# Sums of the heads' outputs by accumulating stores, one ring of six for weight blocks and pooled tiles, and one product order for every pair

## The chip, the cores and the metric

The kernel runs on one core of one Trainium2 chip. The metric is the device time of one execution in microseconds, the median of several runs. TensorE (PE) multiplies, VectorE (DVE) and ScalarE (ACT) make operands and take results, GpSimd (POOL) does small work, SyncE (SP) issues almost all transfers.

## What is computed

The reference is one decoder block on 1024 tokens of width 1024, all in float32:

```python
q, f_pre, i_val, o_gate, pool_v, gate_a, gate_b = split(x @ w_in)
a = HGRN2(q, f, i_val)             # gated recurrence, 8 heads of 128, chunks of tokens
a = (rms_norm(a) * g * sigmoid(o_gate)) @ w_a
b = (causal_mean(pool_v) - pool_v) @ w_pool(per group) * pool_scale
x = LN(alpha * x + (sigmoid(gate_a) * a + sigmoid(gate_b) * b) @ w_out)
x = LN(alpha * x + relu(x @ w_up)**2 @ w_down)
```

## The kernel before

Every large product is done in three passes (high by high, high by low, low by high part), so that float32 accuracy comes from TensorE's faster 32-bit form. `split` (L123) makes the two parts of an operand: ACT casts the high part (L125), DVE subtracts it (L126).

The large products are also done by a seven-product scheme. `pair` (L270) computes two blocks of 128 output columns for both halves of the tokens. From four weight blocks b11, b12, b21, b22 and seven sets of token sums it makes seven **products** p1 to p7. One product (`prod`, L203) is 12 matmuls of 128x512: L208, L210, L211, four times. The products of a pair go into three PSUM banks: **a** takes p1, and later p6, p5 and p3 on top; **c** takes p2; **z** takes p7, and later p4 on top. Between the additions the bank is read: after p1, ACT copies a (`copied`, L276, the copy is L278); after p7 it copies z; after p6 it copies a again; after p5, DVE adds a to the copy of z (`added`, L281, the addition is L282); after p3 the bank holds the last output. The next product onto a bank has to wait until that reading is done.

There are two orders. With `twin` false, p1 p2 p6 p7 p5 p4 p3: the banks alternate. With `twin` true, p1 p2 p7 p4 p6 p5 p3: z twice running, then a three times running; that order is used where `run` (L366) is given two pairs, whose products alternate, so that the banks alternate again (`a_pair`, L1077, and the first two pairs of the up projection, L1257).

The stages, in order:

- the values of the heads (L443 to L583);
- **the recurrence stage** (L1023 to L1034): ORDER (L33) lists inputs of the heads, pooled channels, output gates and gates, each one pair with `twin` false, run alone. After each product `run` advances the generator `recurrence` by one turn (L380), which at two turns of about 8.5 puts the recurrence's small matmuls between the products. In this stage the order of TensorE's instructions is as written (`manual_schedule`, L1025); the other engines' orders, and TensorE's in all other stages, are set by a scheduler when the kernel is built;
- what is left of the recurrence's turns (L1033), then `pool_products` for group 0, `gates(6)`, `pool_products` for groups 1 to 3 and `gates(7)` (L1035);
- the product with w_a on two pairs at a time (L1091 to L1113), for which `o_operand` (L606) loads the heads' outputs and their sums;
- the product with w_out, the first layer norm, the up projection in 16 pairs (L1259 to L1293) and the down projection.

What the change touches besides: `raw_tile` (L213) is a ring of two tiles of 4 KB per partition, two blocks each, and differences of blocks go to a ring "t" of two (L247). The parts of operands go to a ring of 10 tiles, NW, which is five products' worth. `turn_outputs` (L973) stores each head's output of each half to DRAM (L979) from the tile "og", of which there is one; the next half's `outputs` (L955) loads its gate into that same tile (L957). `o_sums` (L614) loads four of those stores back for each of four block rows, makes s3, s2, s1, s4 with four DVE operations (L617 to L620) in tiles of the ring "c", and stores them (L622). The copies L278 of the pairs use ring "c" too. `pool_products` (L717) loads w_pool into "tA" and the pooled tiles into "q", "f", "og" and "v" (L725, L728).

Of the kernel before, what the change touches and what calls it, by code (L numbers as in the profile page):

```python
# [9 lines left out]
F32 = mybir.dt.float32  # L10
# [6 lines left out]
P = 128  # L17
# [18 lines left out]
    ("gates", 2), ("inputs", 7), ("pooled", 3), ("gates", 3), ("gates", 4), ("gates", 5),  # L36
# [14 lines left out]
def tile_hybrid_block(  # L51
# [126 lines left out]

    def first_tokens(name, *tags):
# [33 lines left out]
    def raw_tile():  # L213
        return wq.tile([P, CH, 2, P], F32, tag="raw", name=nm("raw"), bufs=2)

    def w_blocks(src, c1, c2, tile_of=raw_tile):

        raw = tile_of(), tile_of()

        def load(*which):  # L220
            for kh in range(2):
                rows_of = src[kh * HALF : (kh + 1) * HALF, :].rearrange("(k p) c -> p k c", p=P)
                if c2 == c1 + P and len(which) == 2:
                    done = nc.sync.dma_start(
                        out=raw[kh].rearrange("p k n c -> p k (n c)"), in_=rows_of[:, :, c1 : c1 + 2 * P]
                    )
                else:
                    for n in which:
                        c = (c1, c2)[n]
                        done = nc.sync.dma_start(out=raw[kh][:, :, n], in_=rows_of[:, :, c : c + P])  # L230
            return done

        return raw, load

    def loaded_blocks(*args):
        raw, load = w_blocks(*args)
        load(0, 1)
        return raw
# [6 lines left out]

    def w_diff(a, b):
        t = wq.tile([P, CH, P], F32, tag="t", name=nm("t"), bufs=2)  # L247
        V.tensor_sub(t, a, b)  # L248
        return t
# [20 lines left out]
    def pair(raw, rooms, takes, pz_tag="pj", twin=False, pc_tag="pj"):  # L270


        b11, b12, b21, b22 = raw if len(raw) == 4 else (raw[kh][:, :, n] for kh in range(2) for n in range(2))
        c, ps = {}, {}

        def copied(room, ps):  # L276
            t = room()
            A.copy(t, ps)  # L278
            return t

        def added(t, ps):  # L281
            V.tensor_add(t, t, ps)  # L282
            return t

        def t3():
            c["t"] = w_diff(b22, b12)
            return w_part(c["t"])

        def t2():
            if not twin:  # L290
                V.tensor_add(c["t"], c["t"], b11)
            return w_part(c["t"])

        def t4():
            if not twin:
                V.tensor_sub(c["t"], b21, c["t"])
                return w_part(c["t"])
            V.tensor_add(c["t"], c["t"], b11)
            V.tensor_sub(b21, b21, c["t"])
            return w_part(b21)  # L300

        def t1():
            return w_part(w_diff(b12, b11))

        def p1(w):
            ps["a"] = ps_tile()
            prod(ps["a"], w, "a11", True)
            c[11] = copied(rooms[0], ps["a"])

        def p2(w):  # L310
            ps["c"] = ps_tile(pc_tag, 4 if pc_tag == "pj" else 2)
            prod(ps["c"], w, "a12", True)

        def p7(w):
            ps["z"] = ps_tile(pz_tag, 4 if pz_tag == "pj" else 2)
            prod(ps["z"], w, "s3", True)
            with tc.high_priority(PRIO):
                takes[0](added(c[11], ps["c"]))
                c[22] = copied(rooms[2], ps["z"])

        def p6(w):
            prod(ps["a"], w, "s2", False)
            with tc.high_priority(PRIO):
                c[21] = copied(rooms[1], ps["a"])
                if twin:
                    takes[2](added(c[21], ps["z"]))

        def p4(w):
            prod(ps["z"], w, "a22", False)
            if not twin:  # L330
                with tc.high_priority(PRIO):
                    takes[2](added(c[21], ps["z"]))
# [20 lines left out]
        return (  # L353
            ((t0,), ((t0, p1),)),
            ((b_21,), ((b_21, p2),)),
            *(
                (((t3,), ((t3, p7),)), ((t4,), ((t4, p4),)), ((t2,), ((t2, p6),)), ((t1,), ((t1, p5),)))
                if twin
                else (((t3, t2), ((t2, p6), (t3, p7))), ((t1, t4), ((t1, p5), (t4, p4))))
            ),  # L360
            ((b_22,), ((b_22, p3),)),
        )
# [48 lines left out]
    with tc.tile_pool(name="xr", bufs=8, side="right", reuse_waits="tile") as xr:  # L411
# [11 lines left out]
        g_col, pscale = prm[:, 16:24], prm[:, 24:32]  # L423
        lb = const.tile([P, 8], F32, name="lb")
# [29 lines left out]
        def raw_tile_rows():  # L454
            return [raw_tile().rearrange("p k n c -> p (k n c)").rearrange("p (k c) -> p k c", c=HALF) for _ in range(2)]
# [138 lines left out]
    def raw_rows(src, k2, cc):  # L594

        raw = raw_tile().rearrange("p k n c -> p (k n c)").rearrange("p (k c) -> p k c", c=HALF)
        rows_of = src[k2 * P : (k2 + 2) * P, cc * HALF : (cc + 1) * HALF].rearrange("(k p) c -> p k c", p=P)
        nc.sync.dma_start(out=raw, in_=rows_of)
# [15 lines left out]
    def o_sums(kp, tile_of=c_tile):  # L614

        a11, a21, a12, a22 = (loaded(od[k][u], tile_of) for k, u in ((kp, 0), (kp, 1), (kp + CH, 0), (kp + CH, 1)))
        V.tensor_add(a22, a21, a22)  # L617
        V.tensor_sub(a21, a11, a21)
        V.tensor_sub(a11, a22, a11)
        V.tensor_sub(a12, a12, a11)  # L620
        for name, t in zip(("s3", "s2", "s1", "s4"), (a21, a11, a22, a12)):
            nc.sync.dma_start(out=osd[name][kp], in_=t)  # L622

# [3 lines left out]
    with tc.tile_pool(name="tmp", bufs=1, side="right", reuse_waits="tile") as tmp:  # L627
# [89 lines left out]
        def pool_products(g):  # L717

            tags = iter(("q", "f", "og", "v") * 3)

            def room(dtype=F32):
                return tt(next(tags), dtype)

            raw = tt("tA").rearrange("p (k c) -> p k c", c=2 * P)
            nc.sync.dma_start(out=raw, in_=w_pool[g].rearrange("(k p) c -> p k c", p=P))  # L725
            wh, wl = split(raw, lambda: room(F32R).rearrange("p (k c) -> p k c", c=2 * P))
            for u in range(2):
                pl = [split(loaded(pod[2 * g + i][u], room), row_tile) for i in range(2)]  # L728
                for i in range(2):
                    w = slice(i * P, (i + 1) * P)  # L730
                    j = 2 * g + i
                    t = room() if j == KT - 1 else loaded(gbd[j][u], room)
# [88 lines left out]
        class Half:  # L821
# [151 lines left out]
            def turn_outputs(self):  # L973
# [4 lines left out]
                V.scalar_tensor_tensor(self.og, pt, g_col[:, self.h : self.h + 1], self.og, ALU.mult, ALU.mult)  # L978
                nc.sync.dma_start(out=od[self.h][self.u], in_=self.og)  # L979

        def recurrence():
# [10 lines left out]
            for n in range(2 * HEADS + 1):  # L992
# [11 lines left out]
                for turn in range(1, round(at) - round(at - PER_HALF)):  # L1004
                    if turn == TURN_BACK:
# [18 lines left out]
        head_inputs(0, (None, None, "p6", None, None))  # L1024
        with tc.manual_schedule(engines={mybir.EngineType.PE}):  # L1025
# [9 lines left out]
            for what, j in (  # L1035
                ("pool_products", 0), ("gates", 6), ("pool_products", 1), ("pool_products", 2), ("pool_products", 3), ("gates", 7),
# [40 lines left out]
        def a_pair(p):  # L1077
            raw = loaded_blocks(w_a, 2 * p * P, (2 * p + 1) * P, raw_tile if p % 2 else mg_raw)
            room = mg_tile("room", 4)
            takes = [gated(2 * p + i, u, p < 2) for u in range(2) for i in range(2)]  # L1080
            return pair(raw, (c_tile, room, room), takes, "hg", True)
# [76 lines left out]
    with tc.tile_pool(name="wo", bufs=1, side="right", reuse_waits="tile") as mp:  # L1158
        st1 = [None] * 8
        g1, b1 = ln_params(lambda: f(act_tile()).rearrange("p a b -> p (a b)"), ln1_g, ln1_b)  # L1160
        for k2 in range(0, KT, 2):
            raw = raw_rows(w_out, k2, 1)
            for k in range(2):
                n = len(wo)
                out_row(raw[:, k], (
# [46 lines left out]
    with tc.tile_pool(name="up", bufs=1, side="right", reuse_waits="tile") as up:  # L1212
# [15 lines left out]
        def units(i, raw):  # L1228
# [28 lines left out]
            return pair(raw, (c_tile,) * 3, (take(0), last, take(2), take(3)), "hg", i < 2, "tr" if i == 2 else "pj")  # L1257

        def up_blocks(i):  # L1259
            return w_blocks(w_up, i * 2 * P, i * 2 * P + P, up_raw_tile if i % 2 else raw_tile)  # L1260

        blocks = [up_blocks(i) for i in range(2)]
        for _, load in blocks:
            load(0, 1)
        pairs = [units(i, raw) for i, (raw, _) in enumerate(blocks)]
# [21 lines left out]
        for i in range(3, NP):  # L1287
            raw, load = up_blocks(i)
            w_load = load(0, 1)
            if i == NP - 2:  # L1290
                for part in down_rows(0, ws0):
                    part(w_load)
# [185 lines left out]
```

## Time and profile before

| what | value |
|---|---|
| median of the runs | 1476.05 us (1474.28 to 1478.21) |
| the profiled execution's own time | 1478.48 us |
| its span, first to last instruction | 1476.5 us |
| mean granted TensorE clock | 0.991 |
| PE busy | 1439.8 us, 98% |
| DVE busy | 1113.2 us, 75% |
| ACT busy | 759.3 us, 51% |
| POOL busy | 82.3 us, 6% |
| transferred | 226.82 MB, mean 154 GB/s |

The span is 1.98 us shorter than the execution's own time; this lies around it. PE is busy nearly all the time, so the place to look is the remaining 36.7 us in which it is not, and the stretches in which its granted clock is below 1.

### The profile page before, as it was taken

What the parts mean: (1) busy time and instruction counts of PE and PEld (TensorE: products, weight loads), DVE (VectorE), ACT (ScalarE), POOL (GpSimd) and SP (SyncE); (2) the same over time, 40 slices, a digit from 0 to 9 for tenths busy, and PEclk for the clock granted to TensorE, in tenths of its full rate; (3) what the DMA queues carried; (4) which work ended last, traced back from release to release, by engine and by line L of the source; (5) the groups of instructions that cost most, each with busy time, mean ns of one, the idle gap of its engine ahead of it and who ended that gap; (6) DMA issues with size and microseconds to landing.
All of it is one profiled execution on the core that took longest, in us unless ns stands there. A gap on an engine that the chain in (4) does not pass through costs nothing.

```text
span 1476.5 us, 20702 instructions
## 1 busy us (share of the span) xinstructions
PE 1439.8 (98%) x7377; PEld 1191.5 (81%) x7377; DVE 1113.2 (75%) x1822; ACT 759.3 (51%) x1383; POOL 82.3 (6%) x260
## 2 busy tenths in 40 slices
PE   9999999999999998789999999999999999999997
PEld 7887888888878886668788888888888888888886
DVE  5967877887897895458986589666666787777978
ACT  5445566666655654446542357555555543343435
POOL 0002111111110100000002100000000100000000
PEclk9999999999999999999999999999999999999999
DMA  6232233233234336687764134444464874535422
GB/s 249 76 117 93 63 103 122 72 122 122 65 128 160 127 116 220 192 297 271 244 211 160 57 115 164 157 147 151 146 238 168 274 267 135 170 132 169 137 72 114
DMA packets 160615, 226.82 MB, mean 154 GB/s; under 512 B 11232, under 2 KB 84480, under 8 KB 160512
## 3 DMA queue, kind: packets, MB, share of 16 engines
q1 hardware_dynamic: 158576, 218.93, 44.1%
q0 software_dynamic: 1152, 4.19, 0.8%
q10 hardware_dynamic: 784, 2.38, 0.5%
q8 instruction: 58, 0.95, 0.3%
q14 instruction: 45, 0.37, 0.1%
HBM read 154.16 MB, written 71.30 MB: 153 GB/s over the span
## 4 chain that ended last, share of the span: by engine, by line
PE 86%; DVE 6%; DMA 5%; ACT 2%; issue 1%; SPq 0%; DVEq 0%; ACTq 0%
PE ps_pj L208 14%; PE ps_pj L210 14%; PE ps_pj L211 14%; PE ps_pj L1360 4%; PE ps_pj L1361 4%; PE ps_pj L1359 4%; PE ps_pj L113 2%; PE ps_pj L112 2%; PE ps_pj L114 2%; PE ps_tr L1360 1%; PE ps_tr L1361 1%; PE ps_tr L1359 1%; PE ps_sc L208 1%; DMA og<-po 1%; PE ps_sc L211 1%; PE ps_sc L210 1%
## 5 line engine op out<-in xcount | busy, mean ns | idle before, releaser
L208 PE MATMUL ps_pj<-act,w 128*128 128x512 f32 x1068 | 421.8, 396 | 10.3 <-ACT c L278 6.0
L211 PE MATMUL ps_pj<-act,w 128*128 128x512 f32 x1068 | 416.4, 391 | 0.1
L210 PE MATMUL ps_pj<-act,w 128*128 128x512 f32 x1068 | 415.9, 391 | 0.5 <-DVE act L131 0.5
L208 PEld LDWEIGHTS ps_pj<-act,w 128*128 128x128 f32 x1068 | 201.5, 189 | 56.5 <-ACT c L278 7.4
L211 PEld LDWEIGHTS ps_pj<-act,w 128*128 128x128 f32 x1068 | 201.5, 189 | 43.5 <-DVE w L126 0.5
L210 PEld LDWEIGHTS ps_pj<-act,w 128*128 128x128 f32 x1068 | 201.7, 189 | 41.6 <-DVE act L131 0.9
L125 ACT CAST w<-t 128x512 fp32r<-128x512 f32 x170 | 105.7, 622 | 139.0 <-PE ps_pj L210 82.5
L125 ACT CAST w<-raw 128x512 fp32r<-128x512 f32 x143 | 88.7, 622 | 129.0 <-PE ps_pj L210 79.7
L126 DVE TENSOR_TENSOR w<-t,w 128x512 fp32r<-128x512 f32 x170 | 116.3, 686 | 38.1 <-ACT w L125 37.6
L126 DVE TENSOR_TENSOR w<-raw,w 128x512 fp32r<-128x512 f32 x143 | 99.8, 701 | 57.3 <-ACT w L125 56.1
L1321 ACT CAST act<-act 128x1024 fp32r<-128x1024 f32 x66 | 67.0, 1050 | 107.6 <-issue 35.0
L1360 PE MATMUL ps_pj<-act,act 128*128 128x512 f32 x240 | 92.9, 389 | 0.0
L1361 PE MATMUL ps_pj<-act,act 128*128 128x512 f32 x240 | 92.9, 389 | 0.0
L1359 PE MATMUL ps_pj<-act,act 128*128 128x512 f32 x240 | 92.4, 389 | 0.0
L1322 DVE TENSOR_TENSOR act<-act,act 128x1024 fp32r<-128x1024 f32 x66 | 79.2, 1219 | 16.5 <-ACT act L1321 16.4
L282 DVE TENSOR_TENSOR c<-c,ps_pj 128x512 f32<-128x512 f32 x95 | 64.7, 682 | 30.9 <-PE ps_pj L211 24.8
L278 ACT COPY c<-ps_pj 128x512 f32<-128x512 f32 x96 | 55.9, 583 | 16.1 <-PE ps_pj L211 9.1
L248 DVE TENSOR_TENSOR t<-raw,raw 128x512 f32<-128x512 f32 x43 | 29.6, 689 | 37.5 <-DMA raw<-in_w_in_dram 36.4
L1360 PEld LDWEIGHTS ps_pj<-act,act 128*128 128x128 f32 x240 | 45.0, 188 | 9.5 <-DVE act L1322 0.2
L1359 PEld LDWEIGHTS ps_pj<-act,act 128*128 128x128 f32 x240 | 45.0, 188 | 9.4
L1361 PEld LDWEIGHTS ps_pj<-act,act 128*128 128x128 f32 x240 | 45.0, 188 | 9.2
L1225 ACT ACTIVATE c<-c 128x512 f32<-128x512 f32 x61 | 38.6, 633 | 1.7
(418 smaller groups left out, 2722.9 us busy)
## 6 DMA issues: line engine op xcount, KB each, us to landing
h<-c SPq DMA_DIRECT2D x106, 256.0 KB, 2.2
act<-h SPq DMA_DIRECT2D x78, 256.0 KB, 2.9
raw<-in_w_in_dram SPq DMA_DIRECT2D x64, 256.0 KB, 3.6
draw<-in_w_down_dram SPq DMA_DIRECT2D x16, 1024.0 KB, 7.7
raw<-in_w_up_dram SPq DMA_DIRECT2D x30, 512.0 KB, 4.0
raw<-in_w_in_dram SPq DMA_DIRECT2D x18, 512.0 KB, 4.0
hf<-h SPq DMA_DIRECT2D x34, 256.0 KB, 3.0
c<-o SPq DMA_DIRECT2D x24, 256.0 KB, 3.5
```

What stands on the lines that cost most here:

```text
L125: A.copy(hi, src)
L126: V.tensor_sub(lo, src, f(hi))
L208: PE.matmul(ps, wh[:, k], th, start=first and k == 0, stop=False, skip_group_check=True)
L210: PE.matmul(ps, wh[:, k], tl, start=False, stop=False, skip_group_check=True)
L211: PE.matmul(ps, wl[:, k], th, start=False, stop=k == CH - 1, skip_group_check=True)
L278: A.copy(t, ps)
L282: V.tensor_add(t, t, ps)
L1321: A.copy(hi, src)
L1322: V.tensor_sub(lo, src, f(hi))
L1359: PE.matmul(ps, hh[:, w], wh, start=fresh and n == 0, stop=False, skip_group_check=True)
L1360: PE.matmul(ps, hh[:, w], wl, start=False, stop=False, skip_group_check=True)
L1361: PE.matmul(ps, hl[:, w], wh, start=False, stop=n == M - 1, skip_group_check=True)
```

## The change

1. **One product order.** `twin` goes away: every pair, alone or not, runs p1 p2 p7 p4 p6 p5 p3. Differences of blocks are made in place, in the blocks' own tiles and one more tile t. Where z is in the ring "pj", its bank is taken just ahead of the bank of p2 and not with p7.
2. **One ring of six.** Tiles of 2 KB per partition ("raw", six of them) hold one block each; a pair takes five (b11, b21, b12, t, b22, in this order). Loads of w_up and of the neighbouring blocks of w_in become transfers of 256 KB with rows of 512 bytes; before, two neighbouring blocks came in one transfer of 512 KB.
3. **Pooled tiles in that ring.** `pool_products` loads w_pool and a group's four pooled tiles into it, ahead of the group's products.
4. **Sums by accumulating stores.** `o_sums` goes away. `turn_outputs` stores the output (with the sign turned in the second half of the tokens, `g_neg`) to each of the sums that it belongs to: the first to arrive by a plain store on SP, the later ones by accumulating stores issued by GpSimd. That is 12 plain stores of outputs, 16 plain stores and 28 accumulating stores of sums, in place of 16 stores of outputs, 16 loads and 16 stores of sums. The weights of w_a get the matching signs (`turned`).
5. **`gates(6)`** moves to the end of ORDER, ahead of all `pool_products`.

```diff
-    ("gates", 2), ("inputs", 7), ("pooled", 3), ("gates", 3), ("gates", 4), ("gates", 5),
+    ("gates", 2), ("inputs", 7), ("pooled", 3), ("gates", 3), ("gates", 4), ("gates", 5), ("gates", 6),
...
-        return wq.tile([P, CH, 2, P], F32, tag="raw", name=nm("raw"), bufs=2)
+    def block_tile(shape=(CH, P)):
+        return wq.tile([P, *shape], F32, tag="raw", name=nm("raw"), bufs=6)
...
+    def loaded_blocks(src, c1, c2, done=None):
+
+        raw = {}
+        for i in ((0, 0), (1, 0), (0, 1), "t", (1, 1)):
+            raw[i] = block_tile(), None
+            if i != "t":
+                raw[i] = wide_block(src, i[0], (c1, c2)[i[1]], raw[i][0])
...
+        def t4():
+            if turned:
+                V.tensor_sub(b12, b11, b12)
+                minus_sum(c["t"], b22, b12)
+                minus_sum(b21, c["t"], b21)
+            else:
+                V.tensor_sub(b12, b12, b11)
+                V.tensor_sub(c["t"], b22, b12)
+                V.tensor_sub(b21, b21, c["t"])
+            return w_part(b21)
...
         def p2(w):
+            if pz_tag == "pj":
+                ps["z"] = ps_tile()
             ps["c"] = ps_tile(pc_tag, 4 if pc_tag == "pj" else 2)
...
-            *(
-                (((t3,), ((t3, p7),)), ((t4,), ((t4, p4),)), ((t2,), ((t2, p6),)), ((t1,), ((t1, p5),)))
-                if twin
-                else (((t3, t2), ((t2, p6), (t3, p7))), ((t1, t4), ((t1, p5), (t4, p4))))
-            ),
...
+            for operand, product in ((t0, p1), (b_21, p2), (t3, p7), (t4, p4), (t2, p6), (t1, p5), (b_22, p3))
...
+    FIRST = {(0, 0): ("s3", "s2", "s4"), (0, 1): ("s1",), (1, 0): (), (1, 1): ()}
+    ONTO = {(0, 0): (), (0, 1): ("s3", "s2", "s4"), (1, 0): ("s4",), (1, 1): ("s2", "s1", "s4")}
+
+    def put_output(h, u, t):
+
+        right, kp = divmod(h, CH)
+        if (right, u) != (0, 1):
+            nc.sync.dma_start(out=od[h][u], in_=t)
+        for name in FIRST[right, u]:
             nc.sync.dma_start(out=osd[name][kp], in_=t)
+        for name in ONTO[right, u]:
+            nc.gpsimd.dma_start(out=osd[name][kp], in_=t, accum_op=ALU.add)
...
+            raw = loaded(w_pool[g].rearrange("(k p) c -> p k c", p=P), lambda: block_tile((2, 2 * P)))
+            pods = [[loaded(pod[2 * g + i][u], lambda: block_tile((HALF,))) for i in range(2)] for u in range(2)]
...
-                V.scalar_tensor_tensor(self.og, pt, g_col[:, self.h : self.h + 1], self.og, ALU.mult, ALU.mult)
-                nc.sync.dma_start(out=od[self.h][self.u], in_=self.og)
+                gain = (g_neg if self.u else g_col)[:, self.h : self.h + 1]
+                V.scalar_tensor_tensor(self.og, pt, gain, self.og, ALU.mult, ALU.mult)
+                put_output(self.h, self.u, self.og)
...
-                        if old and old.u and old.h >= CH:
-                            last = old.h == HEADS - 1
-                            tags = iter(("tD", "tE", "tF", "tC"))
-                            o_sums(old.h - CH, (lambda: tt(next(tags))) if last else c_tile)
...
-                ("pool_products", 0), ("gates", 6), ("pool_products", 1), ("pool_products", 2), ("pool_products", 3), ("gates", 7),
+                ("pool_products", 0), ("pool_products", 1), ("pool_products", 2), ("pool_products", 3), ("gates", 7),
```

More of the change, by code (lines that the diff above doesn't have):

```diff
@@ L268, in c_late, with pair @@
         return c_tile(False)
-    def pair(raw, rooms, takes, pz_tag="pj", twin=False, pc_tag="pj"):
-        b11, b12, b21, b22 = raw if len(raw) == 4 else (raw[kh][:, :, n] for kh in range(2) for n in range(2))
+    def pair(raw, rooms, takes, pz_tag="pj", pc_tag="pj", turned=False):
+        b11, b12, b21, b22, t = raw if len(raw) == 5 else (*raw, None)
         c, ps = {}, {}
@@ L314, in p7 @@
         def p7(w):
[L315 removed]
+            if pz_tag != "pj":
+                ps["z"] = ps_tile(pz_tag, 2)
             prod(ps["z"], w, "s3", True)
@@ L1255, in last @@
                 put(6, s4)
[L1257 to L1265, printed above, removed]
+            return pair(raw, (c_tile,) * 3, (take(0), last, take(2), take(3)), "hg", "tr" if i == 2 else "pj")
+        blocks = loaded_blocks(w_up, 0, P), wide_blocks(w_up, 2 * P, up_raw_tile)
+        pairs = [units(i, raw) for i, raw in enumerate(blocks)]
         run(pairs[0][1:2])
```

110 lines of the change are left out of this document (41 added, 69 removed).

## The prediction

> **What bounds the kernel now.** I read the page first, then the table by windows, then what TensorE waited for, and last single instructions.
>
> ```profile
> span 1476.5 us, 20702 instructions
> PE 1439.8 (98%) x7377; PEld 1191.5 (81%) x7377; DVE 1113.2 (75%) x1822; ACT 759.3 (51%) x1383; POOL 82.3 (6%) x260
> PE   9999999999999998789999999999999999999997
> ```
>
> TensorE is the bound: 1476.5 - 1439.8 = 36.7 us of the span are without a matmul, and only slices 16 to 18 of 40, about 550 to 675 us, show less than 9. The windows (width, then busy us of PE, PEld, DVE, ACT, POOL, then granted clock, DMA share and GB/s) say the same:
>
> ```profile
> core 0: us, PE busy (x) PEld busy (x) DVE busy (x) ACT busy (x) POOL busy (x), PEclk, DMA share, GB/s
> 250.00:275.00 25.00, 25.00 (x177) 21.18 (x176) 19.49 (x39) 16.64 (x37) 3.85 (x14) 1.00 0.31 103
> 600.00:625.00 25.00, 17.41 (x71) 13.42 (x70) 12.34 (x20) 11.29 (x27) 0.00 (x0) 0.86 0.65 208
> 614.00:617.00 3.00, 3.00 (x7) 1.96 (x8) 2.29 (x4) 0.25 (x1) 0.00 (x0) 0.50 0.94 295
> 617.00:620.00 3.00, 3.00 (x13) 2.15 (x12) 2.60 (x5) 2.51 (x5) 0.00 (x0) 0.92 0.90 259
> 650.00:675.00 25.00, 23.47 (x94) 18.48 (x94) 18.39 (x30) 13.53 (x25) 0.00 (x0) 0.93 0.96 330
> ```
>
> The first row stands for the recurrence stage (some 130 to 600 us): TensorE full, nothing hidden to be had back. The pool stage waits, with the DMA engines near full, and after a long gap the clock is halved (0.50). What TensorE waited for (us in total, times, longest):
>
> ```profile
> PE ps_pj L112 <- ACT w L125: 7.6, 1, 7.6
> PE ps_pj L208 <- ACT c L278: 6.0, 2, 5.6
> PE ps_pj L112 <- ACT q L125: 3.4, 2, 3.0
> PE ps_pj L208 <- DVE c L282: 1.9, 1, 1.9
> ```
>
> The second is the copy of a bank (L278) late because its c tile was still being read by o_sums (L619). The chain and TensorE's timeline there:
>
> ```profile
> 562.28 0.70 DVE c L619
> ...
> 563.00 0.59 ACT c L278
> ```
> ```profile
> 544.65 0.39 PE L211 MATMUL ps_pj<-act,w 128*128 128x512 f32 x1
> ...
> 548.06 0.39 PE L211 MATMUL ps_pj<-act,w 128*128 128x512 f32 x1
> ...
> 557.60 0.39 PE L211 MATMUL ps_pj<-act,w 128*128 128x512 f32 x1
> 563.64 0.79 PE L208 MATMUL ps_pj<-act,w 128*128 128x512 f32 x1 [5.65 <-ACT c L278]
> ...
> 569.75 0.40 PE L211 MATMUL ps_pj<-act,w 128*128 128x512 f32 x1
> ...
> 613.78 0.80 PE L112 MATMUL ps_pj<-w,q 128*128 128x512 f32 x1 [7.59 <-ACT w L125]
> ```
>
> **What the change takes away.** (1) With o_sums gone, that c tile is free. From 557.60 to 569.75 TensorE made 15 steps in 12.15 us; at the usual step of 3.41 / 15 = 0.227 us (544.65 to 548.06) they take 3.4. Gain 8.7. (2) The 7.59 us at 613.78 are pool_products waiting for the recurrence's last turns to give back og. With gates(6) ahead of them, the built order puts five of its products behind the last of these turns, 5 x 2.72 = 13.6 us of cover. Gain 7.6, plus the slow clock after it, 3.00 x 0.50 + 3.00 x 0.08 = 1.7: 9.3. What is late next is the transfers: a pool group moves 13 tiles of 256 KB (w_pool, four pooled, four gates, four stores; two gates fewer in the last), 13.1 MB in all, for 4 x 24 matmuls of 0.227 = 21.8 us of TensorE.
>
> ```profile
> 645.00:649.00 4.00, 1.49 (x7) 0.91 (x5) 1.37 (x3) 1.27 (x3) 0.00 (x0) 1.00 0.99 340
> ```
>
> At 340 GB/s that is 38.5 us, and 2 MB for gates(6) add 6. Between the start of gates(6) and the end of the pool products TensorE has 19 + 22 = 41 us of work, so some 4 us or more of waiting stay even if the ring loads well ahead; today it is 3.4 (L112 <- q) and a little slow clock, about 6. I take no difference, bounds -6 to +6. Together: -18.0.
>
> **What it adds: the order of the products.** This is the large term. Today no product in the built order follows one onto the same bank directly. In the changed kernel's built order 52 do, nearly all in the recurrence stage, where TensorE's order is as written: p4 directly onto p7's z, p5 onto p6's a, p3 onto p5's a. Of these, 35 wait for ACT's copy (L278) of the bank just filled, 17 (p3) for DVE's addition (L282). At 14 more the recurrence's own matmuls lie between. In the up projection the scheduler still alternates two pairs, so no meeting arises there; the w_a pairs keep their order.
>
> ```profile
> L282 DVE TENSOR_TENSOR c<-c,ps_pj 128x512 f32<-128x512 f32 x95 | 64.7, 682 | 30.9 <-PE ps_pj L211 24.8
> L278 ACT COPY c<-ps_pj 128x512 f32<-128x512 f32 x96 | 55.9, 583 | 16.1 <-PE ps_pj L211 9.1
> ```
> ```profile
> 592.68 0.39 PE L211 MATMUL ps_pj<-act,w 128*128 128x512 f32 x1
> ```
> ```profile
> 593.10 0.59 ACT L278 COPY c<-ps_pj 128x512 f32<-128x512 f32 x1 [1.31 <-PE ps_pj L211]
> ```
> ```profile
> 886.48 0.62 ACT L125 CAST w<-raw 128x512 fp32r<-128x512 f32 x1
> 887.00 0.58 ACT L278 COPY c<-ps_sc 128x512 f32<-128x512 f32 x1
> ```
> ```profile
> 428.69 0.58 ACT L278 COPY f<-ps_pj 128x512 f32<-128x512 f32 x1
> ```
> ```profile
> 429.33 0.50 PE L208 MATMUL ps_pj<-act,w 128*128 128x512 f32 x1 [0.80 <-ACT f L278]
> 429.66 0.40 PE L210 MATMUL ps_pj<-act,w 128*128 128x512 f32 x1
> ```
>
> Let T be the start of a product's last matmul. An ACT that waits for nothing else starts the copy at T + 0.42 (592.68 to 593.10), it takes 0.58, and TensorE goes on 0.06 after its end (428.69 + 0.58 to 429.33): T + 1.06. The usual next start is T + 0.23, and the first matmul after a wait takes 0.33 instead of 0.23 (429.33 to 429.66). So a meeting costs 1.06 - 0.23 + 0.10 = 0.93 us at least. But in the built order a cast (L125) of the operand five products on stands directly ahead of nearly each of these copies, and it waits for the last matmul but one of this very product, which frees its room in the ring of ten. It starts at T + 0.20, the next on ACT 0.52 later (886.48 to 887.00), so the copy at T + 0.72: 1.23 us. I take 1.23: 35 x 1.23 = 43.1.
>
> For the addition the same sum with 0.68 gives 1.03 us if DVE is idle, up to 2 if it has a backlog; between p5's start and its end 2.7 us of DVE work at hand (the cast's low part, the addition into c21, two differences, parts of the recurrence) about fill the time. I take 1.25: 17 x 1.25 = 21.3. The 14 covered ones: nothing to 0.5 each, I take 3 in all, since the matmuls between take 1.2 us or more. Sum +67.4.
>
> **The other edits** cost nothing as far as TensorE's waits go.
> - o_sums takes 16 DVE operations of 0.70 away; TensorE waited for them only at 563.64, counted above.
> - GpSimd gets 28 accumulating stores.
>
> ```profile
> L1369 POOL DMA_DIRECT2D act<-x x7: 528/530/722, 1160.5 to 1170.7; - x7
> ...
> DMA to landing us min/median/max: 4.9/7.3/8.6
> ```
> ```profile
> o<-og SPq DMA_DIRECT2D x16, 256.0 KB, 2.2
> ```
>
> Three of them take 3 x 0.53 us of GpSimd, which is 6% busy and whose next work in a half comes later than they do. They hold the one og tile for about 1.6 + 7.3 = 8.9 us; the next half needs it at its turn 0, which is 4.5 products, 12 us, later. But SP issues in order, and the load into og waits at its head: rival 3.
> - The ring of six: loads are spread more evenly, and five products stay as cover:
>
> ```profile
> DVE t L248 <- DMA raw<-in_w_in_dram: 36.4, 20, 4.7
> ACT w L125 <- DMA raw<-in_w_in_dram: 13.3, 7, 2.5
> ```
>
> These waits don't reach TensorE today. In the changed kernel a late load would, since the copy stands behind a cast; but the slot of b22 is now freed five products ahead of its use and not two. Smaller rows for w_up raise the DMA share in a stage in which TensorE waits for nothing.
>
> **The clock.** One window each behind a gap that cost the clock (1.94 us at 131.48) and with one that did not (0.80 us at 429.33, above):
>
> ```profile
> 131.48 0.50 PE L208 MATMUL ps_pj<-act,w 128*128 128x512 f32 x1 [1.94 <-DVE c L282]
> ```
> ```profile
> 133.00:135.00 2.00, 2.00 (x6) 1.53 (x6) 2.00 (x6) 1.27 (x4) 0.00 (x0) 0.50 0.34 124
> ...
> 428.00:431.00 3.00, 2.20 (x10) 1.51 (x9) 3.00 (x9) 2.81 (x9) 0.16 (x1) 1.00 0.23 87
> ```
>
> So gaps of 0.8 us keep the clock, of 1.9 us lose it; the new ones are 1.0 (1.36 - 0.39) to 1.3, and I take it that they keep it. The Trainium skill (TensorE: Matmul & The Clock Gate, "HAM oscillation — how this bites in real kernels") asks only that no gap be longer than about 3.4 us; by this the new gaps are harmless, but the first row here shows 0.50 after 1.9 us already.
>
> **Rivals.**
> 1. *The clock goes at each row of meetings.* For: they come three to a pair. Against: each gap is nearer to 0.8 than to 1.9. Six matmuls in 2 us at clock 0.50 lose 2.00 x 0.5 = 1.0 us, and such a stretch lasts some 3.2 us: 1.6 us for each of 23 pairs, +37: 1562. The Trainium skill has this as "A second HAM failure mode: psum-queue depth-cycling" on the same page: many short idles between groups of matmuls make the clock swing. No run here has yet shown it.
> 2. *The meetings are covered and the kernel is faster.* The point is 18.0 / 52 = 0.35 us for a meeting: below it the gains win. For: 14 of 66 are covered already. Against: the copy alone takes 0.58. Fully covered: 1476.05 - 18.0 = 1458.
> 3. *SP stands still behind the accumulating stores.* Twelve halves have them; each holds SP's head for some 8.9 us where a plain store took 2.2. If a third of these 12 x 6.7 us reach TensorE through late loads and blocked casts, +27: 1552.
> 4. *No difference:* the gains need not depend on the order, but 52 meetings at 0.35 exactly is a narrow place: near 1476.
>
> **The numbers.** 1478.48 - 18.0 + 67.4 = 1527.9 for the profiled execution; the median of the runs lies 2.43 us below it, so 1525.4. The forecast's own range: every meeting at its floor (52 x 0.95 = 49) and pool waits cleared (-6) give 1501; a DVE backlog of 1 us at 17 and 6 more in the pool stage give 1549. Chances: forecast 0.67, rival 1 0.13, rival 2 0.06, rival 3 0.12, rival 4 0.02. The range to hold 8 in 10 reaches from 1502 up into rivals 3 and 1: to 1556. A measurement of this kernel can tell about 0.3% from no change. Faster by more than that: rival 2, 0.06; within: 0.02; slower: 0.92.
>
> **What would show it.** PE busy at 85 to 92% in windows between 150 and 550 us where it is 100% now, with waits of L211 for L274 (the copy's new line) and for L278 (the addition's), about 35 and 17 times, 0.9 to 1.2 us each; clock 1.00 there. No 5.65 us wait near the end of the recurrence and no 7.59 ahead of the pool products. The up projection as before. The prediction is wrong if these waits are few or below 0.35 us, if the clock falls to 0.50 among them, or if ACT and DVE show waits for raw or og of many us in that stage.

## The result, and the profile after

| kernel | median, us | lowest to highest | ratio to before, 95% interval |
|---|---|---|---|
| before | 1476.57 (4 runs) | 1474.28 to 1478.21 | |
| changed | 1569.28 (4 runs) | 1567.09 to 1573.95 | 1.0633 (1.0605 to 1.0661) |

The change makes the kernel 92.7 us slower. The forecast was 1525.4, with a range up to 1556.0: the sign was right, the size was not. Here is the head of the changed kernel's page. In it and all later views of it the three lines of `prod` are L211, L213 and L214, the copy is L274, the addition L278, the accumulating stores L618.

```profile
span 1567.2 us, 20891 instructions
PE 1479.0 (94%) x7377; PEld 1189.9 (76%) x7377; DVE 1105.1 (71%) x1807; ACT 761.3 (49%) x1383; POOL 106.4 (7%) x288
PE   8998988888999899899999999999999999999997
```

The span grew by 90.7 us. TensorE's time without a matmul grew from 36.7 to 88.2, and most of the new waiting lies in the first 17 slices, up to about 665 us, in the recurrence stage. But *busy* PE time grew as well, from 1439.8 to 1479.0, with the same 7377 matmuls. A part of that comes with the waits: the first matmul behind each takes longer, the last one ahead of it ends later than its step, and the clock is slow behind the longest. e5 below, which has the waits and not the second cause, shows 1458.3. The other 20.7 us need a second cause. What TensorE waited for (us in total, times, longest):

```profile
PE ps_pj L211 <- ACT c L274: 34.5, 30, 2.9
PE ps_pj L211 <- DVE c L278: 13.5, 11, 2.6
PE ps_pj L211 <- ACT f L274: 10.0, 6, 4.0
PE ps_pj L211 <- DVE f L278: 8.8, 6, 3.3
```

36 waits for the copy and 17 for the addition, 66.8 us, where 35 and 17 were forecast. The single waits of 5.65 and 7.59 us of the kernel before are not among the answers. A plain meeting, on ACT and then on TensorE:

```profile
237.00 0.62 ACT L125 CAST w<-raw 128x512 fp32r<-128x512 f32 x1 [2.48 <-PE ps_pj L213]
237.52 0.58 ACT L274 COPY c<-ps_pj 128x512 f32<-128x512 f32 x1
```
```profile
238.16 0.50 PE L211 MATMUL ps_pj<-act,w 128*128 128x512 f32 x1 [0.96 <-ACT c L274]
...
238.72 0.39 PE L214 MATMUL ps_pj<-act,w 128*128 128x512 f32 x1
...
240.81 0.40 PE L214 MATMUL ps_pj<-act,w 128*128 128x512 f32 x1
```

The cast released by the last matmul but one, the copy 0.52 behind it, TensorE idle for 0.96: this is the meeting as it was forecast (1.23 less the 0.10 of the first step and the 0.16 by which the last matmul's row outlasts its step, 0.39 against 0.23). And one that is not plain:

```profile
291.07 0.39 PE L214 MATMUL ps_pj<-act,w 128*128 128x512 f32 x1
295.41 0.50 PE L211 MATMUL ps_pj<-act,w 128*128 128x512 f32 x1 [3.95 <-ACT f L274]
295.75 0.46 PE L213 MATMUL ps_pj<-act,w 128*128 128x512 f32 x1
...
299.39 0.39 PE L213 MATMUL ps_pj<-act,w 128*128 128x512 f32 x1
```
```profile
292.45 1.28 ACT L666 ACT_TABLE_LOAD   x1
293.74 0.63 ACT L666 ACTIVATE q<-c 128x512 f32<-128x512 f32 x1
294.28 0.60 ACT L125 CAST w<-raw 128x512 fp32r<-128x512 f32 x1
294.79 0.58 ACT L274 COPY f<-ps_pj 128x512 f32<-128x512 f32 x1
```

The copy could start at 291.5 and starts at 294.79: ACT first works off what the recurrence and the previous pair have put into its queue, a table load of 1.28 us among it. After this gap the clock is gone for a while: the nine steps from 295.75 to 299.39 take 3.64 us, where nine of 0.233 are 2.10. The windows show where it is granted and where not (width, busy us of PE, PEld, DVE, ACT, POOL, then clock, DMA share, GB/s):

```profile
250.00:275.00 25.00, 23.08 (x163) 18.52 (x162) 16.77 (x33) 13.97 (x33) 3.86 (x14) 1.00 0.42 135
296.00:297.80 1.80, 1.80 (x6) 1.40 (x5) 0.50 (x2) 0.00 (x0) 0.22 (x2) 0.50 0.53 153
1050.00:1075.00 25.00, 25.00 (x108) 20.06 (x107) 14.87 (x23) 12.60 (x22) 0.00 (x0) 1.00 0.38 127
```

Six such slow stretches lie in the recurrence stage (behind waits of 2.2 to 3.95 us), each worth 1.1 to 1.6 us; before there were two in this stage, behind the waits at 131.48 and 563.64. Ordinary meetings keep the clock, as forecast (250 to 275).

The last row is the second cause. In the up projection TensorE is busy without a gap at full clock in both kernels, and yet 25 us hold 108 matmuls, where those of the kernel before hold 112:

```profile
1050.00:1075.00 25.00, 25.00 (x112) 20.67 (x111) 16.94 (x26) 14.58 (x25) 0.00 (x0) 1.00 0.46 158
```

From one matmul to the next it is 0.233 us (238.72 to 240.81 above are nine steps in 2.09 us) and not 0.227. In the down projection, where both operands come from tiles named act, the step is 0.227 in both kernels. `prod` makes 3696 matmuls (44 pairs of seven products of 12); at 0.006 more each that is about 22 us that no wait shows. Most of the experiments below look for where it comes from.

### The profile page after: what moved, and what is told of

The parts are those of the page before. It is cut to its first block, busy times and chain, and to the rows that moved or that the text cites. A ratio compares the mean times of both kernels' runs of the same rounds, so it can differ in the third digit from the quotient of the medians.

```text
span 1567.2 us, 20891 instructions
## 1 busy us (share of the span) xinstructions
PE 1479.0 (94%) x7377; PEld 1189.9 (76%) x7377; DVE 1105.1 (71%) x1807; ACT 761.3 (49%) x1383; POOL 106.4 (7%) x288
## 4 chain that ended last, share of the span: by engine, by line
PE 54%; DMA 2%; DVE 2%; ACT 1%; issue 0%; DVEq 0%; ACTq 0%; SPq 0%
PE ps_pj L211 7%; PE ps_pj L214 7%; PE ps_pj L213 7%; PE ps_pj L1348 4%; PE ps_pj L1350 4%; PE ps_pj L1349 4%; PE ps_pj L113 2%; PE ps_pj L114 2%; PE ps_pj L112 2%; PE ps_tr L1348 1%; PE ps_tr L1350 1%; PE ps_tr L1349 1%; PE ps_hg L211 1%; PE ps_sc L211 1%; PE ps_hg L213 1%; PE ps_sc L213 1%
## 5 line engine op out<-in xcount | busy, mean ns | idle before, releaser
L211 PE MATMUL ps_pj<-act,w 128*128 128x512 f32 x1068 | 434.8, 407 | 69.7 <-ACT c L274 34.5
L214 PE MATMUL ps_pj<-act,w 128*128 128x512 f32 x1068 | 424.1, 398 | 1.2 <-DVE w L126 1.2
L213 PE MATMUL ps_pj<-act,w 128*128 128x512 f32 x1068 | 423.8, 398 | 0.1
L125 ACT CAST w<-raw 128x512 fp32r<-128x512 f32 x327 | 202.0, 621 | 386.6 <-PE ps_pj L213 281.7
L126 DVE TENSOR_TENSOR w<-raw,w 128x512 fp32r<-128x512 f32 x327 | 223.9, 688 | 212.2 <-ACT w L125 209.9
L211 PEld LDWEIGHTS ps_pj<-act,w 128*128 128x128 f32 x1068 | 202.2, 189 | 140.4 <-ACT c L274 47.3
L214 PEld LDWEIGHTS ps_pj<-act,w 128*128 128x128 f32 x1068 | 202.3, 189 | 51.5 <-DVE w L126 2.0
L213 PEld LDWEIGHTS ps_pj<-act,w 128*128 128x128 f32 x1068 | 202.9, 190 | 45.9 <-DVE act L131 0.6
L278 DVE TENSOR_TENSOR c<-c,ps_pj 128x512 f32<-128x512 f32 x95 | 64.9, 683 | 31.3 <-PE ps_pj L214 30.3
L274 ACT COPY c<-ps_pj 128x512 f32<-128x512 f32 x96 | 55.8, 581 | 5.0 <-PE ps_pj L214 3.3
L283 DVE TENSOR_TENSOR raw<-raw,raw 128x512 f32<-128x512 f32 x43 | 29.6, 689 | 20.8 <-DMA raw<-in_w_in_dram 18.9
L1219 ACT ACTIVATE c<-c 128x512 f32<-128x512 f32 x61 | 38.5, 633 | 1.5
L1218 ACT ACTIVATE c<-c 128x512 f32<-128x512 f32 x46 | 29.1, 632 | 13.8 <-DVE c L278 13.6
L618 POOL DMA_DIRECT2D s<-og x28 | 24.9, 1162 | 145.8 <-DVE og L973 145.8
```

The source lines that it names most:

```text
L125: A.copy(hi, src)
L126: V.tensor_sub(lo, src, f(hi))
L211: PE.matmul(ps, wh[:, k], th, start=first and k == 0, stop=False, skip_group_check=True)
L213: PE.matmul(ps, wh[:, k], tl, start=False, stop=False, skip_group_check=True)
L214: PE.matmul(ps, wl[:, k], th, start=False, stop=k == CH - 1, skip_group_check=True)
```

## The experiments

Theories at the start. **A:** the time is the meetings, larger than forecast (queues ahead of the copies), and something about the new constant `g_neg` slows each matmul. `g_neg` takes 32 bytes per partition, so in the built program the tiles act (here the moving operand, 512 columns in a matmul) lie 32 bytes higher, while w (the stationary one, 128 by 128, placed from the other end of the memory) stays. **B:** the step is slower from other traffic, of the smaller transfers or the accumulating stores. **C:** the slow sums come from SP standing behind those stores (rival 3).

**e1: g_neg with 128 bytes**, so that act is aligned to 128 bytes again:

```diff
-        g_neg = const.tile([P, 8], F32, name="g_neg")
+        g_neg = const.tile([P, 32], F32, name="g_neg")[:, :8]
```


> The changed kernel with g_neg taking 128 bytes per partition and not 32, so that the tiles behind it start at multiples of 128 again. Address theory: the 32 bytes of g_neg moved the act tiles to 32 past a multiple of 64, and this alone made the step of the large products 0.233 us where it was 0.227; some 4000 matmuls x 0.006 = 24 us come back: 1545. Rival (the step is slower because the ring of operand parts moved by 4 KB, or because of the transfers): no difference, 1569. The meetings on one bank stay in both: about 53 waits, 67 us.

Measured: 1571.28 us, ratio 1.0630 (1.0608 to 1.0651), step 0.2325. No change: act's alignment is not the cause.

**e2: the kernel before with a constant that nothing uses:**

```diff
+        const.tile([P, 8], F32, name="g_neg")
```


> The kernel before with nothing but one more constant of 32 bytes per partition ahead of the act tiles (never used). Address theory: every stage up to the down projection steps at 0.233 us: 1476 + 24 = 1500. Rival: 1476, and the step stays 0.227.

Measured: 1499.45 us, ratio 1.0141 (1.0124 to 1.0158): 32 bytes that no instruction touches cost 21.6 us. TensorE busy rises, its idle time does not; the up projection's window answers to those above:

```profile
PE 1463.3 (98%) x7377; PEld 1190.3 (79%) x7377; DVE 1115.5 (74%) x1822; ACT 760.4 (51%) x1383; POOL 83.0 (6%) x260
```
```profile
1050.00:1075.00 25.00, 25.00 (x109) 20.09 (x108) 15.15 (x25) 13.91 (x25) 0.00 (x0) 1.00 0.46 156
```

Theory B falls: this kernel has neither the small transfers nor the accumulating stores.

**e3: the changed kernel with the old order** (p1 p2 p6 p7 p5 p4 p3) for the pairs that run alone, g_neg as in e1:

```diff
+        if alone:
+            return (
+                ((t0,), ((t0, p1),)),
+                ((b_21,), ((b_21, p2),)),
+                ((t3, t2), ((t2, p6), (t3, p7))), ((t1, t4), ((t1, p5), (t4, p4))),
+                ((b_22,), ((b_22, p3),)),
+            )
```


> The changed kernel with aligned tiles and, for the pairs of the recurrence stage and the gates, the order p1 p2 p6 p7 p5 p4 p3, in which the banks alternate; all else of the change is in. Order theory: the 52 meetings go, and with them about 67 us of waits, 12 of drain and restart and 9 of slow clock: 1545 - 85 = 1460, below the kernel before. If the accumulating stores or the ring of six cost time as well, it stays above 1476; if waits have other causes, above 1500.

Measured: 1486.9 us, ratio 1.0056 (1.0038 to 1.0074): the order is worth 84.4 us against e1. The step stays 0.233.

**e4: the kernel before with the new order everywhere**, nothing else:

```diff
+        twin = True
...
-        head_inputs(0, (None, None, "p6", None, None))
+        head_inputs(0, (None, None, "p6", None, None, None, None))
```


> The kernel before with the order p1 p2 p7 p4 p6 p5 p3 for every pair, and nothing else of the change: 51 meetings. Order theory: 1476 + 67 (waits) + 12 + 9 = 1560 or a little less. By the sum of the prediction (1.23 and 1.25 us a meeting) 1476 + 67 = 1543. If the meetings cost only together with the ring or the accumulating stores: near 1500.

Measured: 1555.07 us, ratio 1.0524 (1.0502 to 1.0547), +77.2 us. The meetings by themselves, in the old rings and with o_sums, make most of the change's loss.

**e5: the changed kernel with g_neg in an unused part of e01**, a tile that is there anyway, so that nothing moves:

```diff
-        g_neg = const.tile([P, 8], F32, name="g_neg")
+        g_neg = e01[:, 8:16]
```


> The changed kernel with g_neg in the unused half of e01, so that no constant is added and act and every tile behind it stand where they stood in the kernel before. Taking 128 bytes for g_neg gave nothing back, so it is not the multiple of 64 or 128 that counts. Address theory in its new form (the distance between the act tiles and the tiles of the operand parts, modulo 2048 or so, sets the step): here the distance is that of before, step 0.227, 1569 - 23 = 1546. Rival (the ring of operand parts, 4 KB higher, or something else in the change sets the step): 0.233 and 1569.

Measured: 1552.75 us (1552.58 to 1553.57), ratio 1.0507 (1.0484 to 1.0529): 16.5 us less than the changed kernel, the step back at 0.2275. TensorE's busy time falls by 20.7 us, and its time without a matmul grows by 4.6 (88.2 to 92.8):

```profile
PE 1458.3 (94%) x7377; PEld 1191.9 (77%) x7377; DVE 1103.4 (71%) x1807; ACT 761.5 (49%) x1383; POOL 106.7 (7%) x288
```

**e6: the changed kernel with 32 bytes less of the unused space ahead of w** (`pad_top`, 24 floats to 16): w moves up by the 32 bytes by which act moved.

```diff
-    G.memset(pad.tile([P, 24], F32, name="pad_top"), 0.0)
+    G.memset(pad.tile([P, 16], F32, name="pad_top"), 0.0)
```


> The changed kernel with g_neg as it is (act 32 bytes higher) and the pad at the other end of the memory 32 bytes smaller, so that the tiles of the operand parts are 32 bytes higher as well. If the distance between the two counts: step 0.227 and 1546, as with g_neg in e01. If the place of act by itself counts: step 0.233 and 1569.

Measured: 1553.26 us, ratio 1.0504 (1.0479 to 1.0529), like e5. So it is the *distance* of act and w, not the place of either.

**e11 and e12: the kernel before with other distances**, by `pad_top` alone. e11:

```diff
-    G.memset(pad.tile([P, 24], F32, name="pad_top"), 0.0)
+    G.memset(pad.tile([P, 88], F32, name="pad_top"), 0.0)
```


> The kernel before with 256 bytes more of unused memory at the end, so that the operand parts w lie 1280 bytes above act modulo 2048 and not 1536 (nothing else differs). Theory A (fast only where the distance is a multiple of 512): a matmul step of 0.233 us up to the down projection and 1499 us, as with the 32 bytes of e2. Theory B (a multiple of 256 is enough): 0.2275 us and 1477. Theory C (only the exact distance of before is fast, or the step grows with the difference): more than 1499.

e12 has the edit of e6, in the kernel before:

> The kernel before with 32 bytes less of unused memory at the end, so that w lies 1568 bytes above act modulo 2048, 32 bytes off to the other side than in e2 (1504). Theory: any distance that is off costs the same, 0.233 us a step and 1499 us. Rival: only a shorter distance costs, 0.2275 us and 1477.

Measured: e11 1476.62 us, ratio 0.9997 (0.9987 to 1.0006); e12 1499.21 us, ratio 1.0150 (1.0133 to 1.0166). First e11's, then e12's window of the up projection:

```profile
1050.00:1075.00 25.00, 25.00 (x112) 20.68 (x112) 15.44 (x24) 13.79 (x24) 0.00 (x0) 1.00 0.50 168
```
```profile
1050.00:1075.00 25.00, 25.00 (x109) 20.14 (x108) 14.68 (x23) 14.73 (x25) 0.00 (x0) 1.00 0.47 155
```

The multiple of 512 that the first theory asked for is not needed. What the runs show together, with the start of w less the start of act in the built program, modulo 2048:

| distance, bytes | kernels | step |
|---|---|---|
| 1280 | e11 | 0.227 |
| 1536 | before, e4 to e10 | 0.227 |
| 1408 | e1, e3 | 0.233 |
| 1504 | changed, e2 | 0.233 |
| 1568 | e12 | 0.233 |

The fast ones are multiples of 256, the slow ones are not, on both sides and however far off. These five distances are all that was tried.

**e7: old order and g_neg in e01**, that is, the edits of e3 (without its 128 bytes) and of e5 together; the change without its two costs:

> The changed kernel without both costs: banks alternating in the recurrence stage and the gates, and g_neg in e01. If the two add up: 1487 - 22 = 1465, about 12 us below the kernel before, which is what is left of the gains of 18 (no wait on a c tile held by o_sums, pool products covered). If what the first alternating run kept above 1476 has another cause, near 1487.

Measured: 1467.86 us (1465.01 to 1468.64), ratio 0.9928 (0.9904 to 0.9951): it beats both kernels. Against e5 the order alone is 84.9 us. The longest wait of TensorE that is left:

```profile
PE ps_pj L211 <- ACT w L125: 4.1, 1, 4.1
```

**e9: e5 with nine operand parts in the ring (`NW = 9`)**. With ten, the cast ahead of a copy waits for the last matmul but one; with nine it waits for later things, and the copy may go first. This tests the prediction's cast term.

```diff
-NW = 10
+NW = 9
```


> e5 (1552.75 us, the changed kernel without the 32 added bytes) with the ring of operand parts at nine tiles and not ten. With ten, a room comes free at the last matmul but one of a product, and the cast of a later operand stands ahead of the bank's copy on ACT and waits for it; with nine, that cast waits for the product's last matmul itself or for DVE, and in the built order the copy mostly stands ahead of it. Theory (the prediction's term for the cast, 0.29 us of each plain meeting that waits for ACT, about 35 of them): the usual wait of TensorE for the copy falls from 0.96 to about 0.67 us, some -10 us in all, 1543. Rival A: the wait is not made of the cast: it stays at 0.96 and the time at 1553. Rival B: with operands only four products ahead new waits for casts and differences come, 1553 to 1575 with waits of TensorE for w.

Measured: 1541.18 us (1536.44 to 1542.97), 11.6 less than e5. A plain meeting of e9, on ACT and on TensorE:

```profile
270.54 0.58 ACT L274 COPY c<-ps_pj 128x512 f32<-128x512 f32 x1 [3.22 <-PE ps_pj L214]
271.02 0.62 ACT L125 CAST w<-raw 128x512 fp32r<-128x512 f32 x1
```
```profile
270.11 0.39 PE L214 MATMUL ps_pj<-act,w 128*128 128x512 f32 x1
271.18 0.50 PE L211 MATMUL ps_pj<-act,w 128*128 128x512 f32 x1 [0.68 <-ACT c L274]
```

The copy stands ahead of the cast, starts 0.43 after the start of the last matmul and not 0.72, and the usual wait is 0.68 and not 0.97: the 0.29 of the prediction, to the hundredth. In e9's table of waits those for the copy are 23.0 and 4.3 us, against 36.2 and 10.8 in e5's; those for the addition grew, 18.6 and 12.1 against 13.8 and 9.0, since now the low part stands ahead of it on DVE:

```profile
PE ps_pj L211 <- ACT c L274: 23.0, 29, 1.6
PE ps_pj L211 <- DVE c L278: 18.6, 12, 3.2
PE ps_pj L211 <- DVE f L278: 12.1, 7, 3.8
PE ps_pj L211 <- ACT f L274: 4.3, 5, 1.6
```
```profile
PE ps_pj L211 <- ACT c L274: 36.2, 30, 3.4
PE ps_pj L211 <- DVE c L278: 13.8, 11, 2.6
PE ps_pj L211 <- ACT f L274: 10.8, 6, 4.2
PE ps_pj L211 <- DVE f L278: 9.0, 6, 3.3
```

Of the 19.7 us that the copies gained, 35 meetings at 0.29 are 10.2. In the rest the longest waits went as well, from 4.2 to 1.6, probably because a blocked cast also keeps back all work behind it on ACT; no run tests that alone. The additions lost 7.9. That these rows together (11.8) come so near to the 11.6 measured is in part luck: over the whole kernel TensorE's time without a matmul fell by 9.0 us (92.8 to 83.8) and its busy time by 2.4.

**e8: the kernel before with gates(6) at the end of ORDER**, nothing else:

```diff
-    ("gates", 2), ("inputs", 7), ("pooled", 3), ("gates", 3), ("gates", 4), ("gates", 5),
+    ("gates", 2), ("inputs", 7), ("pooled", 3), ("gates", 3), ("gates", 4), ("gates", 5), ("gates", 6),
...
-                ("pool_products", 0), ("gates", 6), ("pool_products", 1), ("pool_products", 2), ("pool_products", 3), ("gates", 7),
+                ("pool_products", 0), ("pool_products", 1), ("pool_products", 2), ("pool_products", 3), ("gates", 7),
```


> The kernel before with nothing but gates(6) moved to the end of ORDER. Prediction's term: the 7.6 us wait ahead of the pool products and 1.7 us of slow clock go, the waits for transfers in the pool stage stay or grow by up to 6: 1476 - 9 = 1467, between 1461 and 1475. If the pool products run back to back into the DMA limit: above 1476.

Measured: 1477.49 us (10 runs), ratio 1.0004 (0.9991 to 1.0017): no gain. The 7.59 us wait is gone, and others stand in its place:

```profile
PE ps_pj L208 <- ACT c L278: 6.5, 2, 5.9
PE ps_pj L112 <- ACT w L125: 2.9, 1, 2.9
PE ps_pj L112 <- ACT q L125: 2.7, 2, 2.3
PE ps_pj L114 <- DVE f L126: 2.6, 2, 1.9
```

The first row is the wait that o_sums makes, as before. With the pool products back to back, their operands (L112 to L114) come late seven times, for 9.6 us, where they came late five times, for 12.0, in the kernel before. From 600 to 760 us TensorE's waits add up to 11.8 us, where they were 12.7, and the clock is at 0.50 for 10.2 us in both.

**e10: e7 with o_sums back** in place of the accumulating stores (the weights of w_a unturned again):

```diff
-                gain = (g_neg if self.u else g_col)[:, self.h : self.h + 1]
-                V.scalar_tensor_tensor(self.og, pt, gain, self.og, ALU.mult, ALU.mult)
-                put_output(self.h, self.u, self.og)
+                V.scalar_tensor_tensor(self.og, pt, g_col[:, self.h : self.h + 1], self.og, ALU.mult, ALU.mult)
+                nc.sync.dma_start(out=od[self.h][self.u], in_=self.og)
...
+                        if old and old.u and old.h >= CH:
+                            last = old.h == HEADS - 1
+                            tags = iter(("tD", "tE", "tF", "tC"))
+                            o_sums(old.h - CH, (lambda: tt(next(tags))) if last else c_tile)
```


> e7 (1467.86 us, alternating order) with o_sums back in place of the accumulating stores (plain gain, 16 loads, 16 DVE operations, 16 stores). The prediction's gain (1), 8.7 us for the c tile that o_sums holds: the 5.65 us wait of TensorE for a copy comes back near the end of the recurrence, 1476 to 1477. Rival: with other ring tags the wait falls elsewhere or is hidden, 1468. Rival 3 of the prediction (accumulating stores hold SP): the kernel gets faster without them, below 1466.

Measured: 1478.99 us (10 runs), ratio 1.0005 (0.9996 to 1.0015): 11.1 us more than e7. Not all of this is the one wait: e10's trace also has three slow stretches of the clock in the pool stage, where e7's has one. The wait is back at its old place, and its releaser is the third operation of o_sums (L627 here):

```profile
566.85 0.79 PE L211 MATMUL ps_pj<-act,w 128*128 128x512 f32 x1 [6.18 <-ACT c L274]
```
```profile
566.21 0.58 ACT L274 COPY c<-ps_pj 128x512 f32<-128x512 f32 x1 [5.11 <-DVE c L627]
```

Theory C falls too: without the accumulating stores the kernel is slower.

## Why the prediction was wrong, step by step

The runs cut the change into four parts, from before to e10, e7, e5 and the changed kernel:

| part | forecast | measured |
|---|---|---|
| ring of six, pooled tiles, gates(6), new order in the up projection (e10 less before) | -9.3, bounds -15.3 to -3.3 | +1.3 |
| o_sums away (e7 less e10) | -8.7 | -11.1 |
| product order (e5 less e7) | +67.4 | +84.9 |
| 32 bytes more between act and w (changed less e5) | not seen | +16.5 |

**The step that failed: a term is missing.** "The other edits cost nothing as far as TensorE's waits go" was true of the waits and not of the time. A new constant was counted as an instruction on DVE and not as a change of every later tile's address. The forecast took the step of 0.227 us from the trace of before as a constant; e2, e5, e6 and e12 show that it depends on where two tiles lie: 16.5 to 21.6 us. Nothing in the trace of before could give the size. That the addresses had changed could be seen in the built program. Without this term the time, 1552.75 in e5, would have lain inside the range, but only in the part that had been added for rivals 3 and 1.

**The term that was mis-sized: the meetings.** Count (52, found 53), place (recurrence stage only, none in the up projection) and the plain wait (0.96; e9 confirms even its parts) were right. The forecast took 1.23 us for a meeting on ACT, 0.97 of it waiting; the waits of the changed kernel average 66.8 / 53 = 1.26. Of the 53, some 15 are clearly longer than plain ones, up to 3.95: 66.8 - 53 x 0.97 = 15.4 us. The six slow stretches behind the longest add some 8. e5 and e7, whose difference the 84.9 is, give the same picture: TensorE is without a matmul for 92.8 us against 30.8, and busy for 1458.3 against 1435.9. Of these 62.0 and 22.4 us, 53 plain meetings make 53 x 0.97 = 51.4 and 53 x 0.26 = 13.8. The other 10.6 are waits that are longer than plain, less those that e7 has of its own; the other 8.6 are about what the slow clock adds. The forecast named a backlog for DVE's additions and priced it; for ACT it took "an ACT that waits for nothing else", and the recurrence has long runs of ACT work, with table loads, at fixed places of each half. In e9, where the casts mostly no longer hold up the copies, the longest of these waits shrink; how much of each is the casts and how much the recurrence is not separated. e4 gives 77.2 for the same order in the old rings.

**Right:** the gain at 563.64, given back by e10 at the same place: 11.1 us (the runs leave some 4 either way) for 8.7, with a wait of 6.18 for 5.65, though slow clock in the pool stage has a part in it; and the clock at plain meetings.

**The gain ahead of the pool products did not come as such.** The cover of five products works (the 7.59 us are gone in e8, e10, e7 and the changed kernel), but what is late next, taken as no difference, took it all back in e8; e10, 1.3 us above the kernel before, agrees. In e7 the pool stage runs at the limit of the transfers (width, busy us, clock, DMA share, GB/s):

```profile
640.00:660.00 20.00, 14.50 (x51) 9.95 (x51) 13.57 (x22) 9.91 (x17) 0.00 (x0) 0.93 1.05 376
```

The prediction's own sum, 44.5 us of transfers for 41 us of TensorE, pointed there; its loss was set against waits that were no longer the last. The changed kernel's table of waits has none for a part of an operand (w) above 1.2 us; why it has none and e7 one of 4.1 is left open.

**The rivals.** Rival 1 (the clock goes at each row of meetings) came nearest in time, 1562, but not as the mechanism: the clock is 1.00 through plain meetings and lost in the recurrence stage only behind six long waits. The Trainium skill's "A second HAM failure mode: psum-queue depth-cycling" (TensorE: Matmul & The Clock Gate), by which many short idles make the clock swing, is thus not borne out for idles of 1 us. Rival 3: SP does wait behind the accumulating stores, 57.1 us in all (L596 for s<-og, 15 times, up to 7.8 us), but TensorE's table of waits has none by a late load in that stage, and e10 is slower without these stores. Rival 2 is refuted by e4, e5 and e7; rival 4 by the result.

## What to carry to other kernels

Before an order of products is changed for a simpler code, ask which bank each one meets and what stands on the reading engine ahead of the reader: the plain wait can be worked out to a hundredth, but the mean is set by the other work in that in-order queue. When a change adds or resizes any tile, compare the addresses of the operands of the hot matmuls as well as the instructions; a longer *busy* time at the same count of matmuls and at clock 1.00 is the sign to look for. And take a good part out of a bad change: accumulating stores in place of a load, add and store round trip, in the old order and with no tile moved, gave 0.7% over the kernel before (e7; with the old round trip, e10, there is no difference).

## What the runs showed of the hardware that was not expected

- The step of a 128x512 matmul depends on the distance of its two operands in the memory: 0.227 us at distances of 1280 and 1536 bytes modulo 2048, 0.233 at 1408, 1504 and 1568. That the loading of weights and the stream of the moving operand get in each other's way at the slow distances is a guess; no run shows the mechanism. The Trainium skill (TensorE: Matmul & The Clock Gate, "Step-by-step: what each phase is for") says that two independent read ports let the next weights load without taking from the running matmul; by that alone the distance would not matter, and 21.6 us in e2 say that it does.
- No single length of a gap parts a kept clock from a lost one. Waits of up to 1.48 us in the changed kernel and one of 1.70 in e7 keep it; 1.82 us in e7 lost it; in the changed kernel 2.08 us at 362.39 and 2.85 us at 649.15 kept it, and 2.22 at 156.29 lost it. The 3.4 us of the Trainium skill (same page, "HAM oscillation — how this bites in real kernels") are too many for this kernel. The traces show what parts these cases: where the gap falls. The six slow stretches of the changed kernel start at 138.92, 155.99, 224.25, 295.94, 326.65 and 528.04, each is 3.41 us long, and from one start to the next it is 5, 20, 21, 9 and 59 times 3.413 us. So they lie in cells of one grid. Of the 2.22 us, 1.92 fall into one cell, and the clock is 0.50 in the next. The 2.85 us are cut by an edge into 1.21 and 1.64 (the 2.08 into 0.47 and 1.60), and the clock stays 1.00. These two cells, each with the one behind it:

```profile
152.58:155.99 3.41, 1.49 (x7) 0.88 (x5) 3.41 (x8) 1.62 (x4) 0.00 (x0) 1.00 0.27 77
155.99:159.40 3.41, 3.11 (x7) 2.48 (x8) 2.43 (x6) 0.85 (x3) 0.32 (x3) 0.50 0.26 74
...
647.51:650.92 3.41, 1.77 (x8) 1.45 (x9) 1.83 (x3) 1.59 (x3) 0.00 (x0) 1.00 0.41 133
650.92:654.33 3.41, 3.41 (x57) 3.01 (x56) 0.69 (x1) 1.13 (x5) 0.00 (x0) 1.00 0.33 100
```

In e7 the 1.82 us and the 1.70 us each lie within one cell. First the 1.70, then the 1.82, again with the cell behind:

```profile
431.75:435.16 3.41, 1.71 (x8) 1.12 (x7) 3.41 (x13) 2.95 (x9) 0.52 (x2) 1.00 0.00 0
435.17:438.58 3.41, 3.41 (x16) 2.81 (x15) 3.41 (x8) 2.70 (x5) 0.10 (x1) 1.00 0.21 77
261.09:264.50 3.41, 1.59 (x7) 1.04 (x6) 3.20 (x8) 3.38 (x7) 0.20 (x2) 1.00 0.12 34
264.50:267.91 3.41, 3.41 (x9) 2.63 (x9) 1.40 (x3) 0.86 (x2) 0.10 (x1) 0.50 0.42 119
```

In these cases the border is thus near half a cell of idle TensorE. Over the traces of all runs it is not sharp: single cells with 1.50 us (e10) and 1.59 (e8) lost the clock, and others with 1.87 (the end of e7) and 1.90 (e5) kept it.

- An accumulating store of 256 KB holds GpSimd for 1.16 us, where 0.53 was taken from plain loads of 512 KB, and lands after 6.1 us (median), against 2.6 of the plain store of the same tile:

```profile
L618 POOL DMA_DIRECT2D s<-og x28 | 24.9, 1162 | 145.8 <-DVE og L973 145.8
...
s<-og POOLq DMA_DIRECT2D x28, 256.0 KB, 6.1
...
s<-og SPq DMA_DIRECT2D x16, 256.0 KB, 2.6
```
